# Where the sums of weight tiles are made in a split-precision encoder trunk: nine additions on GpSimd for six accumulating transfers and three VectorE additions, and three small moves before them

## The chip, the cores and the metric

The program runs on one core of a Trainium2 chip. The metric is the device time of one execution, in microseconds (us), as the median of several; a profiled execution leaves a page and a trace. The engines are TensorE (PE, with its weight loads as PEld), VectorE (DVE), ScalarE (ACT), GpSimd (POOL) and SyncE (SP). SP issues transfers only; POOL issues transfers too, those that add to their destination among them. Names such as L347 are lines of the kernel before. The changed kernel has the same lines further down: by 1 from L45, by 7 from L274 on, so that L347 is L354 there; the sums that were L296 and L306 are L276 as additions and L278 as transfers.

## The reference

A trunk of two encoder layers, for 512 tokens of width 1024, all in f32:

```
for i in range(2):
    h = rmsnorm(x, norm_g[i]);  mem_h = rmsnorm(mem, mem_norm_g[i])     # mem: 256 tokens
    if i == 0: proj = h @ w_in_a;  o_mix = dilated window attention (3 window groups, 8 heads)
    else:      proj = h @ w_in_b;  o_mix = grouped-query attention with axial rotary
    o_mem = attention of 4 heads into mem_h @ w_mem_kv[i]
    x = x + (concat(o_mix, o_mem) * silu(gate)) @ w_out[i]
```

Nearly all of its arithmetic is the product of tokens by weights: `mem_h @ w_mem_kv` first, then `h @ w_in_a` and so on.

## The kernel before

**Three products for one.** PE multiplies in a rounded f32 form (fp32r). Every operand is therefore split in a high part and the rest, a = ah + al and w = wh + wo, and each product becomes ah·wh (L178), al·wh (L179) and ah·wo (L182), added in PSUM. The first two are issued in pairs for four slices of the contraction, and then the four of L182. A weight tile `wl` of 128x1024 f32 comes by a transfer; ACT makes `wh` from it by a cast (L333), and DVE `wo = wl - wh` (L347). For the memory tokens' weights both multiply by a gain as well (L331, L345). `wh` and `wo` lie in rings of four, and the tokens' parts (`act`, `h`, `hS`) are made in the same way by L166 on ACT and L169 on DVE.

**Chunks and sums of weights.** The weights come in chunks of columns. A chunk of the token projections is computed by a Strassen scheme: instead of eight products of quarter blocks, seven, of sums of token blocks (`fS`, `hS`, L650 to L685) with sums of weight blocks 11, 12, 21, 22:

- T1 = 12 + 11, one DVE addition of two SBUF tiles (L291)
- T2 = 22 + T1, a transfer from SBUF to SBUF that adds to its destination, issued by POOL (L296)
- T3, loaded as 12, to which a second transfer from DRAM adds the block of 22, issued by POOL (L260)
- T4 = 21 + T2, again such a transfer (L306), into the tile of 21 once its parts are taken

The chunks are run in the order 1, 2, 0, 3, ...: 1 and 2 are the memory's keys and values, with four plain pieces each, and need no sums. Chunk 0 is the first Strassen chunk, with two tiles of each kind (14 weight pieces); chunk 3 is the second, with one of each (7). The pieces are used in the order 21, 11, T1, T2, 22, T3, T4.

**What sets the order.** It is written out by the program: a counter `W.g` goes up with each group of matmuls, and a weight's load, cast, low part and sums are issued once their inputs are some groups old (`ripe`). `SUM_AT` keeps the sums of chunk 0 back until group 7 (T1) and 10 (T3). The engines take their queues in order and wait on semaphores. `Driver` steps small generators for the rest: `prep` normalises the four token blocks `x[0..3]`, transposes them on PE (`first_t`, `diffs_t`) and makes their sums.

**Before the first Strassen chunk.** `place_m` transposes a memory block on PE (L589) and splits it, `square` takes the sum of squares of one, and `norm_1` takes the squares of half blocks of a token block, on ACT (L576) or DVE (L574), before POOL makes the factor `rstd` (L535, L536); `norm_2` multiplies (L583, DVE). L709 writes the memory's keys out of PSUM with their factor (DVE), L659 and L660 add a token block in PSUM to one in SBUF, and L683 and L685 subtract among tiles in SBUF.

Of the kernel before, what the change touches and what calls it, by code (L numbers as in the profile page):

```python
# [133 lines left out]
def trunk_kernel(ctx: ExitStack, tc: tile.TileContext, x, mem, wall, norm_g, mem_norm_g, gcol,  # L134
# [65 lines left out]
    class Weights:  # L200
# [61 lines left out]
        def dma(self, most=9):  # L262
            while self.allocs and self.live < KEEP_C.get(self.allocs[0][0][0], KEEP[self.allocs[0][2]]) and most:
# [6 lines left out]
                    self.at[key] = self.g  # L270
                self.load(nc.sync, self.tile[key], d)

        def ripe(self, at, key, force, n=None):
            return key in at and (force or self.g - at[key] >= (LEAD if n is None else n))  # L274

        def sum(self, force=False, want=None):  # L276

            for n, (key, d) in enumerate(self.sums[:8]):  # L278
                if want and key != want:
                    continue  # L280
                c, k, x = key
                if not c and not force and self.g < SUM_AT.get(k, 0):
                    break
                if k == "T1" and c >= T1_DMA:
                    if not self.ripe(self.load_at, key, force):
                        continue
                    self.load(G, self.tile[key], d, accum_op=ALU.add)
                elif k == "T1":
                    if not (self.ripe(self.load_at, key, force, 4 if c in KEEP_C else None) and self.ripe(self.at, (c, "11", x), force)):
                        continue  # L290
                    V.tensor_tensor(self.tile[key], self.tile[key], self.tile[c, "11", x], ALU.add)  # L291
                    self.use((c, "11", x))
                elif k == "T2":
                    if not (self.ripe(self.load_at, key, force) and self.ripe(self.at, (c, "T1", x), force, 1 if c < T1_DMA else None)):
                        continue
                    G.dma_start(self.tile[key], self.tile[c, "T1", x], accum_op=ALU.add)  # L296
                    self.use((c, "T1", x))
                elif k == "T3":
                    if not self.ripe(self.load_at, key, force):
                        continue  # L300
                    self.load(G, self.tile[key], d, accum_op=ALU.add)
                else:
                    if not (self.ripe(self.lo_at, (c, "21", x), force, 1) and self.ripe(self.at, (c, "T2", x), force, T4_AT.get(c))):
                        continue
                    self.tile[key] = self.tile[c, "21", x]
                    G.dma_start(self.tile[key], self.tile[c, "T2", x], accum_op=ALU.add)  # L306
                    self.use((c, "T2", x))
                self.at[key] = self.g
# [297 lines left out]
    def proj_t(act, sels, evac, mid=None):  # L606

        def group(w, u, b, p):
            for k in range(4):
                kk = 4 * u + k  # L610
                mm_early(p, sels[b](act, 0, kk), w[k][0], sels[b](act, 1, kk), w[k][0], kk == 0)
            if mid:
                mid(u, b)
            for k in range(4):
                kk = 4 * u + k
                mm_late(p, sels[b](act, 0, kk), w[k][1], kk == 7)
        chunk(2, len(sels), group, evac)
# [605 lines left out]
    def prep():  # L1223

        for c in range(5):
            if c > 2:
                norm_2(xb[c - 1], n[c - 1], rows["x"])
            if c == 2:
                n[2], n[3] = norm_1(xb[2], 1), norm_1(xb[3], 2)
            if 1 < c < 4:  # L1230
                first_t(H, xb[c - 2], c - 2, by_class, from_rows)
            yield 1

        def forms(c):
# [755 lines left out]
```

## Time and profile before

| | |
|---|---|
| runs | 932.94, 933.12, 933.17 us; median 933.12 |
| profiled execution | 933.17 us, span of the trace 931.4 us |
| TensorE clock granted | 1.0 |
| busy, of the span | PEld 87%, ACT 75%, POOL 39% |
| instructions | 16276 |

Times in the trace are us from the span's start; the 1.8 us between span and execution lie outside the trace. A row of the timeline has the start, the busy time, the engine with line and operation, output and inputs, shapes, a count where like instructions are drawn together, and in brackets the idle time before it with what ended that. Successive operations of one engine may overlap in it by about 0.1 us (an operation's start is less than its duration after the one before). A row of a wait has the waiting group, its releaser, and then the total us, the count and the mean.

The memory's products lie at about 8 to 32 us, chunk 0 at about 32 to 70 us, and chunk 3 after it.

### The profile page before, as it was taken

To read this page: it belongs to the slowest core of one execution; us is meant where nothing else is said; L and a number is where in the kernel's file an instruction comes from. 1 tells how busy PE (TensorE), PEld (TensorE's weight loads), DVE (VectorE), ACT (ScalarE), POOL (GpSimd) and SP (SyncE) were. 2 spreads that over 40 slices of the span, in tenths; PEclk is the share of its full clock that TensorE was granted. 3 is DMA by queue.
4 is the path that set the end of the run, shared out by engine and by line. 5 is a ranking of instruction groups with operands and counts; after the bars stand their busy time and mean duration, and the time that the engine had idled before them with its cause. 6 is when DMAs were issued, how large, how long until landed. Compare 5 with 4: busy or idle time off the path is not lost.

```text
span 931.4 us, 16276 instructions
## 1 busy us (share of the span) xinstructions
PE 924.8 (99%) x5471; PEld 814.7 (87%) x5471; DVE 801.7 (86%) x1457; ACT 695.7 (75%) x1725; POOL 360.5 (39%) x504
## 2 busy tenths in 40 slices
PE   9999999999999999999999999999999999999998
PEld 7789888888888888888889998888988999999886
DVE  6999677879888888979798989999898998789977
ACT  7775789677868686867776767757879887789774
POOL 4411425556564646464746102234252440110122
PEclk9999999999999999999999999999999999999999
DMA  9999948968686778686867899999985687785777
GB/s 351 389 264 331 300 127 218 319 146 247 162 248 166 249 160 271 159 272 135 241 178 207 231 261 271 289 320 331 289 219 114 178 233 178 201 227 116 200 162 181
DMA packets 83179, 212.85 MB, mean 229 GB/s; under 512 B 18960, under 2 KB 25752, under 8 KB 83096
## 3 DMA queue, kind: packets, MB, share of 16 engines
q1 hardware_dynamic: 60744, 141.16, 42.3%
q0 software_dynamic: 20384, 67.12, 39.1%
q10 hardware_dynamic: 1968, 3.54, 1.0%
q8 instruction: 43, 0.70, 0.3%
q14 instruction: 40, 0.33, 0.1%
HBM read 162.96 MB, written 12.65 MB: 189 GB/s over the span
## 4 chain that ended last, share of the span: by engine, by line
PE 91%; DVE 5%; DMA 2%; ACT 1%; SPq 0%; issue 0%; DVEq 0%; ACTq 0%
PE pj L178 24%; PE pj L179 24%; PE pj L182 24%; PE qT L716 3%; PE sa L1476 2%; PE oo L1585 2%; PE ptb L1819 1%; PE sa L1472 1%; DVE wo L347 1%; PE pt L1564 1%; DMA x<-in_x_dram 1%; DMA row<-in_norm_g_dram 1%; PE ob L178 1%; PE ob L182 1%; PE ob L179 1%; PE xT L589 1%
## 5 line engine op out<-in xcount | busy, mean ns | idle before, releaser
L347 DVE TENSOR_TENSOR wo<-wl,wh 128x1024 fp32r<-128x1024 f32 x253 | 308.8, 1225 | 5.6 <-ACT wh L333 5.6
L333 ACT CAST wh<-wl 128x1024 fp32r<-128x1024 f32 x253 | 267.3, 1061 | 27.5 <-PE pj L179 19.5
L178 PE MATMUL pj<-wh,hS 128*128 128x512 f32 (+1 forms) x416 | 154.5, 380 | 0.0
L179 PE MATMUL pj<-wh,hS 128*128 128x512 f32 (+1 forms) x416 | 148.9, 367 | 0.0
L178 PE MATMUL pj<-wh,h 128*128 128x512 f32 (+1 forms) x312 | 115.3, 378 | 0.0
L179 PE MATMUL pj<-wh,h 128*128 128x512 f32 (+1 forms) x312 | 111.6, 367 | 0.0
L536 POOL TENSOR_TENSOR rstd<-mse,half 128x4 f32<-128x4 f32 (+2 forms) x98 | 102.0, 1041 | 8.2
L182 PE MATMUL pj<-wo,hS 128*128 128x512 f32 (+1 forms) x416 | 99.5, 366 | 0.0
L179 PEld LDWEIGHTS pj<-wh,hS 128*128 128x128 f32 x416 | 78.7, 189 | 11.2
L178 PEld LDWEIGHTS pj<-wh,hS 128*128 128x128 f32 x416 | 78.6, 189 | 11.0
L535 POOL TENSOR_SCALAR mse<-hss 128x4 f32<-128x4 f32 (+1 forms) x88 | 45.6, 519 | 104.4 <-ACT junk L704 91.3
L182 PEld LDWEIGHTS pj<-wo,hS 128*128 128x128 f32 x416 | 72.4, 189 | 13.0 <-DVE wo L347 0.2
L704 ACT ACTIVATE junk<-sn 128x128 f32<-128x128 f32 x264 | 79.3, 310 | 3.4 <-DVE sn L428 3.4
L260 POOL DMA_DIRECT2D wl<-in_wall_dram x44 | 41.9, 982 | 95.4 <-DMA wl<-in_wall_dram 21.7
L1417 POOL TENSOR_TENSOR ta<-sn,tabs 128x128 f32<-128x128 f32 (+1 forms) x64 | 38.3, 605 | 104.0 <-DVE sn L709 80.4
L415 ACT COPY sn<-pj 128x512 f32<-128x512 f32 x122 | 67.2, 590 | 12.3 <-PE pj L182 12.3
L182 PE MATMUL pj<-wo,h 128*128 128x512 f32 (+1 forms) x312 | 74.5, 366 | 0.0
L306 POOL DMA_DIRECT2D wl<-wl x35 | 31.0, 895 | 109.2 <-DVE wo L347 48.7
L438 DVE TENSOR_TENSOR sn<-pj,sn 128x512 f32<-128x512 f32 x89 | 60.7, 683 | 6.5 <-PE pj L182 6.2
L179 PEld LDWEIGHTS pj<-wh,h 128*128 128x128 f32 x312 | 59.0, 189 | 8.4
L178 PEld LDWEIGHTS pj<-wh,h 128*128 128x128 f32 x312 | 59.0, 189 | 8.2
L296 POOL DMA_DIRECT2D wl<-wl x35 | 32.9, 964 | 78.7 <-DVE wl L291 18.9
(299 smaller groups left out, 2403.0 us busy)
## 6 DMA issues: line engine op xcount, KB each, us to landing
wl<-in_wall_dram SPq DMA_DIRECT2D x226, 512.0 KB, 7.4
wl<-wl POOLq DMA_DIRECT2D x70, 512.0 KB, 5.9
wl<-in_wall_dram POOLq DMA_DIRECT2D x48, 512.0 KB, 8.6
od<-o SPq DMA_DIRECT2D x9, 256.0 KB, 5.8
x<-in_x_dram SPq DMA_DIRECT2D x4, 512.0 KB
v0r<-sn SPq DMA_DIRECT2D x8, 256.0 KB, 8.5
v0d<-v0r SPq DMA_DIRECT2D x4, 512.0 KB
og<-od ACTq DMA_DIRECT2D x4, 512.0 KB
```

Of the source, the lines that this page charges most:

```text
L178: T.matmul(o, a, b, start=start, stop=False, skip_group_check=True)
L179: T.matmul(o, c, d, start=False, stop=False, skip_group_check=True)
L182: T.matmul(o, a, b, start=False, stop=stop, skip_group_check=True)
L260: queue.dma_start(t, wall[d], **how)
L333: A.copy(wh, self.tile[key])
L347: V.tensor_tensor(wo, self.tile[key], wh.bitcast(F32), ALU.subtract)
L415: A.copy(t_, b_)
L438: V.tensor_tensor(t_, b_, t_, ALU.subtract if q == "12" and late is None else ALU.add)
L535: G.tensor_scalar(e, ss, EPS, None, ALU.add)
L536: G.tensor_tensor(r, e, half[:, 0:n], ALU.pow)
L704: A.activation(jk, p[:, j * 128:(j + 1) * 128], AF.Square, scale=by, accum_out=ss[:, j:j + 1])
L1417: G.tensor_tensor(ta[:, 0:n], xn[:, 0:n, 0:32], ropeA[:, 0, b, s0:s0 + n], ALU.mult)
```

## The change

For the chunks 0 and 3, T1, T2 and T4 are made by an addition on POOL (`G.tensor_tensor` in the new method `add`, and in place of `V.tensor_tensor` for T1): six additions in chunk 0, three in chunk 3. The sums T3 and those of all later chunks stay as they were. Beside it there are three moves: the transposition of the second memory block goes in the first group after two pairs of matmuls instead of four (`mid` is called at k = 1 there), and ahead of a square; of the token blocks 2 and 3, block 2 now has both squares on DVE (one on ACT, one on DVE before), and block 3 both on ACT and one step of `prep` later (both on DVE before).

```
--- before.py
+++ after.py
@@ -42,6 +42,7 @@
 SEQ = [1, 2, 0] + list(range(3, len(PLAN)))
 T4_AT = {4: 4}
 T1_DMA = 15
+POOL_SUMS = 0, 3
 SUM_AT = {"T1": 7, "T3": 10}
 KEEP_C = {0: 14, 3: 14, 4: 12}
 KEEP = {"T2": 8, "T2b": 6, "W3": 10, "W1": 9, "W2": 10, "W2s": 9, "W1bs": 9, "W2c": 9, "W1b": 7, "W2b": 9, "W1o": 7}
@@ -270,6 +271,12 @@
                     self.at[key] = self.g
                 self.load(nc.sync, self.tile[key], d)
 
+        def add(self, c, t, u):
+            if c in POOL_SUMS:
+                G.tensor_tensor(t, t, u, ALU.add)
+            else:
+                G.dma_start(t, u, accum_op=ALU.add)
+
         def ripe(self, at, key, force, n=None):
             return key in at and (force or self.g - at[key] >= (LEAD if n is None else n))
 
@@ -288,12 +295,12 @@
                 elif k == "T1":
                     if not (self.ripe(self.load_at, key, force, 4 if c in KEEP_C else None) and self.ripe(self.at, (c, "11", x), force)):
                         continue
-                    V.tensor_tensor(self.tile[key], self.tile[key], self.tile[c, "11", x], ALU.add)
+                    (G if c in POOL_SUMS else V).tensor_tensor(self.tile[key], self.tile[key], self.tile[c, "11", x], ALU.add)
                     self.use((c, "11", x))
                 elif k == "T2":
                     if not (self.ripe(self.load_at, key, force) and self.ripe(self.at, (c, "T1", x), force, 1 if c < T1_DMA else None)):
                         continue
-                    G.dma_start(self.tile[key], self.tile[c, "T1", x], accum_op=ALU.add)
+                    self.add(c, self.tile[key], self.tile[c, "T1", x])
                     self.use((c, "T1", x))
                 elif k == "T3":
                     if not self.ripe(self.load_at, key, force):
@@ -303,7 +310,7 @@
                     if not (self.ripe(self.lo_at, (c, "21", x), force, 1) and self.ripe(self.at, (c, "T2", x), force, T4_AT.get(c))):
                         continue
                     self.tile[key] = self.tile[c, "21", x]
-                    G.dma_start(self.tile[key], self.tile[c, "T2", x], accum_op=ALU.add)
+                    self.add(c, self.tile[key], self.tile[c, "T2", x])
                     self.use((c, "T2", x))
                 self.at[key] = self.g
                 self.sums.pop(n)
@@ -609,8 +616,8 @@
             for k in range(4):
                 kk = 4 * u + k
                 mm_early(p, sels[b](act, 0, kk), w[k][0], sels[b](act, 1, kk), w[k][0], kk == 0)
-            if mid:
-                mid(u, b)
+                if mid and k == (1 if (u, b) == (0, 0) else 3):
+                    mid(u, b)
             for k in range(4):
                 kk = 4 * u + k
                 mm_late(p, sels[b](act, 0, kk), w[k][1], kk == 7)
@@ -1225,8 +1232,8 @@
         for c in range(5):
             if c > 2:
                 norm_2(xb[c - 1], n[c - 1], rows["x"])
-            if c == 2:
-                n[2], n[3] = norm_1(xb[2], 1), norm_1(xb[3], 2)
+            if 1 < c < 4:
+                n[c] = norm_1(xb[c], 2 * (c == 2))
             if 1 < c < 4:
                 first_t(H, xb[c - 2], c - 2, by_class, from_rows)
             yield 1
@@ -1311,8 +1318,8 @@
     def ahead(u, b):
 
         if (u, b) == (0, 0):
+            place_m(1, 0)
             square(1, 0)
-            place_m(1, 0)
             square(0, 1, False)
             W.hi(True)
             W.hi(True)
```

On POOL's queue, behind the last of the key factors (L770) and ahead of the sums of the third Strassen chunk, before (`wl` with a number is one weight tile; 204 and 206 are 21 of chunk 0, 208 and 210 are 11, 212 and 214 are T1, 216 and 218 are T2, 323 and 325 are T3; from 422 or 434 on they are chunk 3's):

```order
L770 TENSOR_SCALAR rstd_426<-rstd_426,rm_74 128x4
L296 DMA wl_216<-wl_212 128x1024
L296 DMA wl_218<-wl_214 128x1024
L260 DMA wl_323<-in_wall_dram 128x1024
L260 DMA wl_325<-in_wall_dram 128x1024
L306 DMA wl_204<-wl_216 128x1024
L306 DMA wl_206<-wl_218 128x1024
L296 DMA wl_572<-wl_570 128x1024
L260 DMA wl_643<-in_wall_dram 128x1024
L306 DMA wl_434<-wl_572 128x1024
L296 DMA wl_891<-wl_821 128x1024
```

and now:

```order
L298 TENSOR_TENSOR wl_212<-wl_212,wl_208 128x1024
L298 TENSOR_TENSOR wl_214<-wl_214,wl_210 128x1024
L276 TENSOR_TENSOR wl_216<-wl_216,wl_212 128x1024
L276 TENSOR_TENSOR wl_218<-wl_218,wl_214 128x1024
L261 DMA wl_323<-in_wall_dram 128x1024
L261 DMA wl_325<-in_wall_dram 128x1024
L276 TENSOR_TENSOR wl_204<-wl_204,wl_216 128x1024
L276 TENSOR_TENSOR wl_206<-wl_206,wl_218 128x1024
L298 TENSOR_TENSOR wl_570<-wl_570,wl_424 128x1024
L276 TENSOR_TENSOR wl_572<-wl_572,wl_570 128x1024
L261 DMA wl_643<-in_wall_dram 128x1024
L276 TENSOR_TENSOR wl_422<-wl_422,wl_572 128x1024
```

Six issues of transfers are gone from the queue and nine additions in their place; the issues of T3 (L260, now L261) stand behind four additions now, and T1's additions are the first work of the queue there.

On DVE, from the last normalisation of the token blocks on (`xn` are the memory's keys, `wo` the low parts of weight pieces), before:

```order
L583 SCALAR_TENSOR_TENSOR x<-x,rstd,row 128x512 x2
L709 TENSOR_TENSOR xn<-pj,rstd 128x512
L347 TENSOR_TENSOR wo<-wl,wh 128x1024 x2
L709 TENSOR_TENSOR xn<-pj,rstd 128x512
L291 TENSOR_TENSOR wl<-wl 128x1024
L659 TENSOR_TENSOR fS_532<-xT,f_496 128x512
L660 TENSOR_TENSOR fS_533<-f_402,xT 128x512
L169 TENSOR_TENSOR hS_536<-fS_532,hS_536 128x4x128
L347 TENSOR_TENSOR wo<-wl,wh 128x1024 x2
L291 TENSOR_TENSOR wl<-wl 128x1024
L659 TENSOR_TENSOR fS_574<-xT,f_537 128x512
L660 TENSOR_TENSOR fS_575<-f_456,xT 128x512
```

and now:

```order
L590 SCALAR_TENSOR_TENSOR x<-x,rstd,row 128x512 x2
L716 TENSOR_TENSOR xn<-pj,rstd 128x512
L354 TENSOR_TENSOR wo<-wl,wh 128x1024 x2
L716 TENSOR_TENSOR xn<-pj,rstd 128x512
L666 TENSOR_TENSOR fS_532<-xT,f_496 128x512
L667 TENSOR_TENSOR fS_533<-f_390,xT 128x512
L170 TENSOR_TENSOR hS_536<-fS_532,hS_536 128x4x128
L354 TENSOR_TENSOR wo<-wl,wh 128x1024 x2
L666 TENSOR_TENSOR fS_574<-xT,f_537 128x512
L667 TENSOR_TENSOR fS_575<-f_456,xT 128x512
L170 TENSOR_TENSOR hS_536<-fS_574,hS_536 128x4x128
L354 TENSOR_TENSOR wo<-wl,wh 128x1024
```

The two L291 of chunk 0 are gone; every other operation keeps its place. (A third L291, chunk 3's, is gone further on.)

On ACT, where the weight pieces of the memory end (`sq` are squares of a token half block, `h` the high parts of tokens, `junk` squares of memory keys), before:

```order
L331 ACTIVATE wh<-wl,gmc 128x512 x4
L576 ACTIVATE sq,ss<-x 128x512
L166 CAST h_389<-xT 128x4x128
L166 CAST h_395<-xT 128x4x128
L650 COPY f_400<-xT 128x512
L650 COPY f_402<-xT 128x512
L704 ACTIVATE junk,hss<-pj,rm 128x128 x4
L166 CAST h_389<-xT 128x4x128
L166 CAST h_395<-xT 128x4x128
```

and now:

```order
L338 ACTIVATE wh<-wl,gmc 128x512 x4
L167 CAST h_377<-xT 128x4x128
L167 CAST h_383<-xT 128x4x128
L657 COPY f_388<-xT 128x512
L657 COPY f_390<-xT 128x512
L711 ACTIVATE junk,hss<-pj,rm 128x128 x4
L583 ACTIVATE sq,ss<-x 128x512 x2
L167 CAST h_377<-xT 128x4x128
L167 CAST h_383<-xT 128x4x128
```

The cast of the first token block moves ahead of the square, which now stands, with a second one, behind four of the `junk` operations.

More of the change, by code (lines that the diff above doesn't have):

```diff
@@ L44 @@
 T1_DMA = 15
+POOL_SUMS = 0, 3
 SUM_AT = {"T1": 7, "T3": 10}
@@ L271, in dma, with add @@
                 self.load(nc.sync, self.tile[key], d)
+        def add(self, c, t, u):
+            if c in POOL_SUMS:
+                G.tensor_tensor(t, t, u, ALU.add)
+            else:
+                G.dma_start(t, u, accum_op=ALU.add)
         def ripe(self, at, key, force, n=None):
@@ L290, in sum @@
                         continue
-                    V.tensor_tensor(self.tile[key], self.tile[key], self.tile[c, "11", x], ALU.add)
+                    (G if c in POOL_SUMS else V).tensor_tensor(self.tile[key], self.tile[key], self.tile[c, "11", x], ALU.add)
                     self.use((c, "11", x))
@@ L295, in sum @@
                         continue
-                    G.dma_start(self.tile[key], self.tile[c, "T1", x], accum_op=ALU.add)
+                    self.add(c, self.tile[key], self.tile[c, "T1", x])
                     self.use((c, "T1", x))
@@ L305, in sum @@
                     self.tile[key] = self.tile[c, "21", x]
-                    G.dma_start(self.tile[key], self.tile[c, "T2", x], accum_op=ALU.add)
+                    self.add(c, self.tile[key], self.tile[c, "T2", x])
                     self.use((c, "T2", x))
@@ L611, in group @@
                 mm_early(p, sels[b](act, 0, kk), w[k][0], sels[b](act, 1, kk), w[k][0], kk == 0)
-            if mid:
-                mid(u, b)
+                if mid and k == (1 if (u, b) == (0, 0) else 3):
+                    mid(u, b)
             for k in range(4):
@@ L1227, in prep @@
                 norm_2(xb[c - 1], n[c - 1], rows["x"])
-            if c == 2:
-                n[2], n[3] = norm_1(xb[2], 1), norm_1(xb[3], 2)
+            if 1 < c < 4:
+                n[c] = norm_1(xb[c], 2 * (c == 2))
             if 1 < c < 4:
@@ L1313, in ahead @@
         if (u, b) == (0, 0):
+            place_m(1, 0)
             square(1, 0)
-            place_m(1, 0)
             square(0, 1, False)
```

## The prediction

> **What bounds the kernel.** I read the page first: the busy times and the chain of waits by engine.
>
> ```profile
> PE 924.8 (99%) x5471; PEld 814.7 (87%) x5471; DVE 801.7 (86%) x1457; ACT 695.7 (75%) x1725; POOL 360.5 (39%) x504
> PE 91%; DVE 5%; DMA 2%; ACT 1%; SPq 0%; issue 0%; DVEq 0%; ACTq 0%
> ```
>
> TensorE (PE) works 924.8 of 931.4 us and 91% of the chain is PE, so time is won only where PE stands still, and a time that PE loses is not given back. Next, who PE's weight loads and matmuls waited for, over the whole run:
>
> ```profile
> PE xT L589 <- DVE x L583: 1.0, 1, 1.0
> PEld xT L589 <- issue: 1.3, 1, 1.3
> PEld pj L179 <- DVE act L169: 1.3, 3, 0.6
> PEld pj L178 <- ACT wh L331: 0.8, 2, 0.5
> ```
>
> The first two rows are one place, the transposition of the input tokens at 31.64 us, late by 1.0 us (1.3 at the weight load); the other two lie before 15 us. Then the busy time in the stretch that the change touches, in the columns PE, weight load, VectorE (DVE), ScalarE (ACT), GpSimd (POOL):
>
> ```profile
> 34.00:46.00 12.00, 12.00 (x59) 10.01 (x58) 11.69 (x14) 8.41 (x13) 2.88 (x4) 1.00 1.04 378
> 46.00:58.00 12.00, 12.00 (x58) 9.80 (x57) 11.80 (x15) 9.80 (x16) 2.61 (x3) 1.00 1.06 245
> 82.00:94.00 12.00, 12.00 (x103) 12.00 (x102) 8.87 (x11) 6.05 (x15) 3.09 (x4) 1.00 1.05 342
> ```
>
> From 34 to 58 us PE has no hole and DVE rests 0.31 and 0.20 us of 12; only from 82 us on has DVE room (8.87 of 12). How close DVE runs behind PE there, by the timeline:
>
> ```profile
> 53.52 1.22 DVE L347 TENSOR_TENSOR wo<-wl,wh 128x1024 fp32r<-128x1024 f32 x1
> 54.82 1.16 PE L182 MATMUL pj<-wo,hS 128*128 128x512 f32 x4
> ```
>
> The low part `wo` of the seventh weight piece of chunk 0 is ready at 53.52 + 1.22 = 54.74 and PE takes it at 54.82: a margin of 0.08 us. **PE is the bound, and DVE stands right behind it just where the change puts new work on POOL.**
>
> **What the change costs and brings, part by part.**
>
> *The squares and the transposition, before 32 us.* Of the squares of the last two token blocks, one less is on DVE, and the last block's come later, on ACT.
>
> ```profile
> 10.91 0.50 PE L179 MATMUL pj<-wh,act 128*128 128x512 f32 x1 [0.23 <-DVE act L169]
> 22.38 2.62 ACT L331 ACTIVATE wh<-wl,gmc 128x512 fp32r<-128x512 f32 x4 [0.96 <-DMA wl<-in_wall_dram]
> 24.86 0.69 DVE L574 CUSTOM_DVE_ANT_0 sq<-x 128x512 f32<-128x512 f32 x1 [1.10 <-DMA x<-in_x_dram]
> 25.52 1.05 ACT L166 CAST h<-xT 128x512 fp32r<-128x512 f32 x2
> 31.64 1.06 PE L589 MATMUL xT<-ident,x 128*128 128x128 f32 x8 [1.03 <-DVE x L583]
> ```
>
> DVE waited 1.10 us for the last block's transfer before a square, and ACT's cast at 25.52 stood behind a square. Both go: DVE loses the wait and one 0.6 us square, but what it does next needs ACT's cast, which moves up from 25.52 to 25.0 only (ACT's weight casts end there: 22.38 + 2.62). So DVE's queue, and the block that PE waits for at 31.64, come 0.5 to 0.6 us earlier. The two squares on ACT (0.8 each with their read-out) push its next casts to about 30.9; DVE needs them at 31, so they cost nothing. The earlier transposition of a memory block lets ACT and DVE make its tokens sooner; PE waited 0.23 us for such a one at 10.91, but what it wins there it only waits longer at 31.64: the last wait decides. Taken: **-0.6 us**; bounds 0 and -2.4 (every wait above gone).
>
> *Transfers that go.* Nine additions were six accumulating transfers on POOL's queue and three DVE additions.
>
> ```profile
> 52.49 1.05 ACT L333 CAST wh<-wl 128x1024 fp32r<-128x1024 f32 x1 [0.75 <-DMA wl<-wl]
> ```
>
> ACT waited 0.75 us for one such sum, and PE had no hole meanwhile (the row of 46 to 58 us). Worth nothing; bounds 0 and, at most, that 0.75.
>
> *Nine additions of 128x1024 on POOL.* The trace has none of that size; the nearest rows are POOL's products of 128x64 and 128x128:
>
> ```profile
> 178.32 0.46 POOL L1417 TENSOR_TENSOR ta<-sn,tabs 128x128 f32<-128x128 f32 x1 [3.59 <-DVE sn L709]
> 178.74 1.54 POOL L1418 TENSOR_TENSOR tb<-sn,tabs 128x128 f32<-128x128 f32 x1
> 178.75 1.22 DVE L347 TENSOR_TENSOR wo<-wl,wh 128x1024 fp32r<-128x1024 f32 x1
> 179.88 1.48 DVE L291 TENSOR_TENSOR wl<-wl 128x1024 f32<-128x1024 f32 x1
> 199.05 0.68 DVE L438 TENSOR_TENSOR sn<-pj,sn 128x512 f32<-128x512 f32 x1
> 199.21 0.32 POOL L1417 TENSOR_TENSOR ta<-sn,tabs 128x64 f32<-128x64 f32 x1 [3.88 <-DVE sn L709]
> 203.66 1.33 DVE L347 TENSOR_TENSOR wo<-wl,wh 128x1024 fp32r<-128x1024 f32 x1 [1.01 <-ACT wh L333]
> ```
>
> Alone, 64 elements take 0.32 and 128 take 0.46 us: 2.2 ns an element, so 1024 take 0.46 + 896 x 0.0022 = **2.4 us** (an estimate; below it nothing but the 0.46 of the row). The middle rows tell more. L1418 met L347, whose two inputs both lie in SBUF, and took 1.54 instead of 0.46 us: it waited until L347 was done. Then L291, also with two SBUF inputs, took 1.48 instead of 1.22 us: it waited 0.26 us for L1418. So the two exclude each other, for 0.26 / 128 = 2.03 ns an element. L438, whose second input is in PSUM, took its 0.68 us beside a POOL product: it isn't held. For 1024 elements the hold is 2.03 ns x 1024 = **2.08 us**; bounds 0.26 (the lock goes back to DVE piece by piece, and DVE's reads fit between) and 2.4 (the whole instruction).
>
> [...]
>
> *Where the holds fall.* What POOL did and does there:
>
> ```profile
> 31.61 0.60 POOL L770 TENSOR_SCALAR rstd<-rstd,rm 128x4 f32<-128x4 f32 x2
> 38.83 1.08 POOL L296 DMA_DIRECT2D wl<-wl  x1 [6.62 <-DVE wl L291]
> 44.77 2.11 POOL L260 DMA_DIRECT2D wl<-in_wall_dram  x2
> wl<-in_wall_dram POOLq DMA_DIRECT2D x48, 512.0 KB, 8.6
> ```
>
> POOL is free from about 33 us (the row's 32.2, plus the moved norm factor). Before, it then waited 6.62 us for DVE's sum. Now it can start at once, and the next eight additions run back to back, with the two issues of L260 (about 1 us each) after the fourth. Behind those issues stand two pieces of T3: at 2.4 and the 1.1 that an addition waits for an L347, they go out at 33 + 4 x 3.5 = 47 us instead of 44.77, and land 8.6 us later by the median; PE, itself late, takes them after the pieces of T1, T2 and 22, past 58 us. I cost that at nothing (without PE's delay, 2 us). What DVE has to do in the same stretch:
>
> ```profile
> 33.82 0.69 DVE L709 TENSOR_TENSOR xn<-pj,rstd 128x512 f32<-128x512 f32 x1
> 34.42 2.35 DVE L347 TENSOR_TENSOR wo<-wl,wh 128x1024 fp32r<-128x1024 f32 x2
> 36.69 0.69 DVE L709 TENSOR_TENSOR xn<-pj,rstd 128x512 f32<-128x512 f32 x1
> 37.29 1.22 DVE L291 TENSOR_TENSOR wl<-wl 128x1024 f32<-128x1024 f32 x1
> 38.42 0.69 DVE L659 TENSOR_TENSOR fS<-xT,f 128x512 f32<-128x512 f32 x1
> 39.02 0.68 DVE L660 TENSOR_TENSOR fS<-f,xT 128x512 f32<-128x512 f32 x1
> 39.80 0.69 DVE L169 TENSOR_TENSOR hS<-fS,hS 128x512 fp32r<-128x512 f32 x1
> 40.41 2.35 DVE L347 TENSOR_TENSOR wo<-wl,wh 128x1024 fp32r<-128x1024 f32 x2
> 46.13 1.23 DVE L347 TENSOR_TENSOR wo<-wl,wh 128x1024 fp32r<-128x1024 f32 x1 [0.26 <-ACT wh L333]
> 47.28 0.68 DVE L683 TENSOR_TENSOR f<-fS,f 128x512 f32<-128x512 f32 x1
> 48.00 0.69 DVE L685 TENSOR_TENSOR f<-f,f 128x512 f32<-128x512 f32 x1
> ```
>
> If, as at 179.88, the one that waits is let in next, one DVE operation with two SBUF inputs passes between two additions. In order: first addition while L709 (PSUM) runs; L347; second; L347; third, beside L709, L659 and L660 (PSUM); L169; fourth; L347; POOL's two issues, beside them L347; fifth, beside L659 and L660; L169; sixth; L347; seventh; L683; eighth; L685. All eight holds thus fall ahead of the `wo` at 53.52. The sum for DVE there:
>
> - eight holds: 8 x 2.08 = +16.6 us
> - covered by operations on PSUM: 0.6 + 1.8 + 1.2 = -3.6
> - two removed L291, 37.29 to 38.42 each: -2.3
> - DVE's rests of 0.31 and 0.20 in the stretch: -0.5
> - DVE enters earlier by the squares: -0.5
> - margin of 54.82: -0.1
>
> **+9.6 us** for PE, which already contains the -0.6: PE waits for DVE whatever it won before. The chunk's later pieces have wider margins, and the third removed L291 (after 58 us) and the ninth addition (after 73 us, where DVE comes to rest) change nothing. Against the profiled execution's 933.17 (span 931.4 and 1.8 around it; the median of the runs is 933.12): 933.2 + 9.6 = **942.8 us**. With holds of 2.4 it is 945.3; if all eight PSUM operations of that stretch cover (another 1.2) and three holds fall in DVE's gaps, 936.
>
> **Rivals.**
> 1. *No lock that counts.* At 1024 elements POOL reads in pieces and DVE's reads go between, so that an addition costs DVE no more than the 0.26 us of the small one: 8 x 0.26 = 2.1, less than the 2.3 of the removed L291. PE keeps the 0.6 us: 933.2 - 0.6 = 932.6, not slower. For it: no row here is longer than 128 elements. Against it: the hold doubles from 64 to 128 elements (L347 grew by 0.11 at 203.66 beside the small form, L291 by 0.26 beside the large). It decides where a hold is under (2.3 + 3.6 + 1.1) / 8 = 0.9 us, by the terms above.
> 2. *Shared by halves.* The two alternate within an addition, each hold costs DVE half, 1.04 us: 8.3 - 1.8 (cover by halves) - 2.3 - 1.1 = +3.1: 936.3.
> 3. *Faster.* The lock does not count, and fewer transfers bring the weights so early that every later wait of PE goes as well: 933.2 - 0.6 and 1.5 for them = 931.1. Against: none of the groups of waits above names a transfer.
> 4. *The sums don't move at all.* The rows of the order ahead have the additions on POOL and DVE's L291 gone there, so this gets no chance.
>
> **Chances and range.** Forecast 0.68; rival 1: 0.16; rival 2: 0.10; rival 3: 0.06. A measurement of this kernel can tell about 0.2%, 1.9 us, from no change. Faster by more: rival 3, 0.06. Within: rival 1, 0.16. Slower by more: 0.68 + 0.10 = 0.78. The likeliest case alone spans 936 to 946 us (holds of 2.4 and 0.7 for starts that drift); with it and rival 2 alone too much would be left out, so the range reaches down to rival 1: 932.3 to 946.
>
> **What would show it.** Right: L347 (now L354) between 34 and 58 us on average near 2.3 us instead of 1.22, single ones above 3; POOL's additions 2.4 us alone and up to 3.5 where they wait; PE waiting for DVE's `wo` by some 10 us in total before 65 us, the largest single wait 3 to 5 us; DVE without idle time; and from 65 us on the same PE pace as before, later by 9 to 10 us. The start right: PE's wait at 31.64 comes 0.5 earlier. Wrong: L354 stays at 1.22 us beside additions of 2.4 (rival 1), or grows by about 1 us (rival 2). Most of all it would be wrong if DVE is let in more often than one operation per addition.

## The result: 946.4 to 946.9 us, 1.4% slower

| | forecast | measured |
|---|---|---|
| time | 942.8 us (932.3 to 946.0) | 946.91 us median of 4, before 933.14 in the same runs |
| ratio to before | 1.010 | 1.0144 (95% interval 1.0126 to 1.0162) |
| the same kernel once more | | 946.42 us, ratio 1.0138 (1.0121 to 1.0155) |

The direction and the mechanism were right; the loss is 13.8 us where 9.6 were forecast, and the time lies 0.9 us above the range. One of the four executions, the profiled one, took 2386 us, with the matmuls of 512 columns 0.62 us apart instead of 0.23 (without it the median is 946.35), so the profile read here is that of the second series, an execution of 946.61 us with a span of 944.6.

The stretches that the prediction quoted, now (columns as there: PE, weight load, VectorE, ScalarE, GpSimd, then the granted clock of TensorE):

```profile
34.00:46.00 12.00, 9.37 (x43) 6.87 (x41) 11.91 (x7) 6.18 (x10) 12.00 (x6) 1.00 0.98 392
46.00:58.00 12.00, 6.65 (x17) 4.52 (x17) 11.90 (x6) 2.18 (x4) 11.92 (x7) 0.64 0.52 95
58.00:70.00 12.00, 12.00 (x46) 9.71 (x47) 11.93 (x16) 9.79 (x15) 0.24 (x1) 0.79 0.59 140
82.00:94.00 12.00, 12.00 (x75) 10.83 (x75) 11.70 (x11) 6.05 (x8) 3.28 (x2) 1.00 0.67 211
```

VectorE is busy for 11.9 of each 12 us in the first two stretches (11.69 and 11.80 before), but the number of its operations fell from 14 and 15 to 7 and 6: it stands in them. TensorE loses 2.63 us in the first stretch and 5.35 in the second, and its clock, 1.00 throughout before, is 0.64 and 0.79 from 46 to 70 us. The waits of TensorE by groups show whom it waited for:

```profile
PE pj L183 <- DVE wo L354: 7.0, 2, 4.5
PEld pj L183 <- DVE wo L354: 8.3, 3, 4.9
```

Before, no row of the matmuls' waits named `wo`, and the rows of the weight loads came to 0.5 us for it in the whole run; now the low products (ah·wo) wait 7.0 us for it. On VectorE (L354 was L347, L170 was L169, L666 was L659):

```profile
33.92 6.16 DVE L354 TENSOR_TENSOR wo<-wl,wh 128x1024 fp32r<-128x1024 f32 x2
41.97 0.92 DVE L170 TENSOR_TENSOR hS<-fS,hS 128x512 fp32r<-128x512 f32 x1
42.81 3.38 DVE L354 TENSOR_TENSOR wo<-wl,wh 128x1024 fp32r<-128x1024 f32 x1
46.11 9.07 DVE L354 TENSOR_TENSOR wo<-wl,wh 128x1024 fp32r<-128x1024 f32 x1
55.11 0.68 DVE L666 TENSOR_TENSOR fS<-xT,f 128x512 f32<-128x512 f32 x1
56.48 1.50 DVE L170 TENSOR_TENSOR hS<-fS,hS 128x512 fp32r<-128x512 f32 x1
```

and on GpSimd, the eight additions and the two issues between them:

```profile
32.87 6.13 POOL L298 TENSOR_TENSOR wl<-wl 128x1024 f32<-128x1024 f32 x2
38.95 6.15 POOL L276 TENSOR_TENSOR wl<-wl 128x1024 f32<-128x1024 f32 x2
45.05 2.04 POOL L261 DMA_DIRECT2D wl<-in_wall_dram  x2
46.45 5.35 POOL L276 TENSOR_TENSOR wl<-wl 128x1024 f32<-128x1024 f32 x2
51.12 2.98 POOL L298 TENSOR_TENSOR wl<-wl 128x1024 f32<-128x1024 f32 x1
54.17 3.25 POOL L276 TENSOR_TENSOR wl<-wl 128x1024 f32<-128x1024 f32 x1
```

Two L354 that met the first additions took 6.16 us instead of 2.35, L170 took 0.92 and 1.50 instead of 0.69, and L666, with its input in PSUM, the same 0.68 as ever. One L354 took **9.07 us**: it was shut out by the fifth, sixth and seventh addition in a row (46.45 to 54.10).

Where the time stands lost. For each kernel that was run, the table has the start of the first low product of a weight piece, less the same start in the kernel before (from the rows of TensorE in the two traces; the pieces are those that the kernel before starts at 34.39, the last of the memory, 43.45, 46.17, 48.89, 54.82, 71.70 and 106.41 us):

| kernel | 34.39 | 43.45 | 46.17 | 48.89 | 54.82 | 71.70 | 106.41 |
|---|---|---|---|---|---|---|---|
| the change | -0.82 | +2.79 | +9.07 | +12.61 | +13.37 | +13.29 | +13.29 |
| additions alone | -0.21 | +12.70 | +14.91 | +14.94 | +14.93 | +14.85 | +14.85 |
| moves alone | -0.57 | -0.58 | -0.58 | -0.55 | -0.29 | -0.25 | +0.25 |
| chunk 3's three alone | -0.90 | -0.91 | -0.91 | -0.89 | -0.61 | +2.36 | +2.54 |
| chunk 0's six alone | -0.87 | +2.78 | +6.76 | +10.30 | +10.66 | +10.58 | +10.58 |
| holes filled | -0.86 | +3.15 | +9.42 | +10.97 | +11.70 | +11.74 | +11.74 |
| T3 behind the seventh | -0.66 | +2.97 | +3.58 | +6.99 | +12.34 | +12.24 | +12.25 |
| additions in halves | -0.79 | -0.30 | -0.15 | +11.74 | +13.51 | +13.43 | +13.43 |
| T1 on VectorE | -1.04 | -1.04 | -1.04 | +5.60 | +7.36 | +8.01 | +8.56 |
| T1 by transfers | -0.97 | -0.97 | -0.97 | -0.97 | -0.12 | +6.21 | +8.05 |
| squares alone | -1.09 | -1.09 | -1.09 | -1.08 | -0.82 | -0.51 | -0.22 |
| transposition alone | +0.78 | +0.77 | +0.77 | +0.77 | +0.77 | +0.77 | +1.33 |

In the change everything is lost between 34 and 55 us of the kernel before, and from there on TensorE keeps its pace, 13.29 us behind.

### The profile page after: what moved, and what is told of

Same layout as the page of the kernel before. It is cut to its first block, busy times and chain, and to the rows that moved or that the text cites. A ratio compares the mean times of both kernels' runs of the same rounds, so it can differ in the third digit from the quotient of the medians.

```text
span 2384.0 us, 16280 instructions
## 1 busy us (share of the span) xinstructions
PE 2379.3 (100%) x5471; PEld 1712.6 (72%) x5471; DVE 809.6 (34%) x1452; ACT 714.2 (30%) x1727; POOL 331.3 (14%) x507
## 4 chain that ended last, share of the span: by engine, by line
PE 100%; DVE 0%; DVEq 0%; issue 0%; POOL 0%; POOLq 0%
PE pj L180 26%; PE pj L183 26%; PE pj L179 26%; PE qT L723 3%; PE ptb L1826 2%; PE sa L1483 2%; PE oo L1592 2%; PE sa L1479 1%; PE pt L1571 1%; PE xT L596 1%; PE ob L180 1%; PE ob L179 1%; PE ob L183 1%; PE sb L174 1%; PE sb L173 1%; PE sb L175 1%
## 5 line engine op out<-in xcount | busy, mean ns | idle before, releaser
L354 DVE TENSOR_TENSOR wo<-wl,wh 128x1024 fp32r<-128x1024 f32 x253 | 309.3, 1225 | 113.3 <-ACT wh L340 81.7
L179 PE MATMUL pj<-wh,hS 128*128 128x512 f32 (+1 forms) x416 | 328.1, 790 | 0.0
L180 PE MATMUL pj<-wh,hS 128*128 128x512 f32 (+1 forms) x416 | 315.1, 759 | 0.0
L179 PE MATMUL pj<-wh,h 128*128 128x512 f32 (+1 forms) x312 | 245.3, 787 | 0.0
L183 PE MATMUL pj<-wo,hS 128*128 128x512 f32 (+1 forms) x416 | 240.9, 761 | 0.0
L180 PE MATMUL pj<-wh,h 128*128 128x512 f32 (+1 forms) x312 | 236.8, 760 | 0.0
L179 PEld LDWEIGHTS pj<-wh,hS 128*128 128x128 f32 x416 | 155.3, 373 | 68.0 <-issue 59.6
L180 PEld LDWEIGHTS pj<-wh,hS 128*128 128x128 f32 x416 | 155.6, 374 | 65.2 <-issue 65.2
L183 PEld LDWEIGHTS pj<-wo,hS 128*128 128x128 f32 x416 | 143.3, 375 | 77.1 <-issue 73.5
L183 PE MATMUL pj<-wo,h 128*128 128x512 f32 (+1 forms) x312 | 180.3, 759 | 0.0
L180 PEld LDWEIGHTS pj<-wh,h 128*128 128x128 f32 x312 | 117.4, 376 | 49.1 <-issue 49.0
L179 PEld LDWEIGHTS pj<-wh,h 128*128 128x128 f32 x312 | 118.0, 378 | 48.1 <-issue 44.7
L183 PEld LDWEIGHTS pj<-wo,h 128*128 128x128 f32 x312 | 107.7, 372 | 58.0 <-issue 56.7
L422 ACT COPY sn<-pj 128x512 f32<-128x512 f32 x122 | 69.6, 589 | 175.7 <-PE pj L183 175.7
L542 POOL TENSOR_SCALAR mse<-hss 128x4 f32<-128x4 f32 (+1 forms) x88 | 34.3, 390 | 612.3 <-ACT junk L711 600.7
L179 PE MATMUL pj<-hS,wh 128*128 128x256 f32 x192 | 105.4, 555 | 0.0
L180 PE MATMUL pj<-hS,wh 128*128 128x256 f32 x192 | 100.9, 531 | 0.0
```

What stands on the lines that cost most here:

```text
L179: T.matmul(o, a, b, start=start, stop=False, skip_group_check=True)
L180: T.matmul(o, c, d, start=False, stop=False, skip_group_check=True)
L183: T.matmul(o, a, b, start=False, stop=stop, skip_group_check=True)
L354: V.tensor_tensor(wo, self.tile[key], wh.bitcast(F32), ALU.subtract)
L422: A.copy(t_, b_)
```

## The experiments

**The change again, and its two halves.** The first expectation is that of the changed kernel's second series; "Theory L" and "Theory C" are used from here on. Where the expectations speak of a port, the runs show only that an addition on GpSimd and a VectorE operation with two SBUF inputs keep each other waiting (two L354 6.16 us instead of 2.35, above); what lies behind that was not shown.

> The changed kernel once more, for a profile at its usual pace (its first profile caught an execution of 2386 us, in which every matmul took more than twice its time). Theory L, the shared port alone: 946 to 947 us; VectorE is held once for each of eight additions, about 2.1 us each, and TensorE's waits for wo between 34 and 80 us add up to the whole 13.4 us. Theory C, the port and then TensorE's clock: the other runs of this kernel show a granted clock of 0.992 where the kernel before has 1.0, so TensorE's waits add up to only 9 to 10 us, and the other 3 to 4 us lie in matmuls that stand further apart after a wait, in windows with a granted clock below 1.00.

Measured: 946.42 us. Both theories had a part of it. TensorE's holes over 0.15 us up to 60 us add up to 10.2 us (2.23 in the kernel before), so 7.9 us are standing time; the rest of the 13.3 is slow work. Around the two holes, from TensorE's timeline:

```profile
46.24 2.08 PE L183 MATMUL pj<-wo,h 128*128 128x512 f32 x4 [2.47 <-DVE wo L354]
55.24 2.07 PE L183 MATMUL pj<-wo,h 128*128 128x512 f32 x4 [4.50 <-DVE wo L354]
58.51 0.63 PE L180 MATMUL pj<-wh,hS 128*128 128x512 f32 x1
58.94 0.63 PE L179 MATMUL pj<-wh,hS 128*128 128x512 f32 x1
```

and the granted clock in short stretches (the number after the parenthesis of GpSimd):

```profile
46.00:48.00 2.00, 1.76 (x4) 1.48 (x5) 2.00 (x2) 0.00 (x0) 2.00 (x3) 0.51 0.77 113
48.00:50.00 2.00, 2.00 (x7) 1.54 (x7) 2.00 (x1) 0.00 (x0) 2.00 (x2) 0.64 1.00 199
50.00:52.00 2.00, 0.74 (x4) 0.27 (x2) 2.00 (x1) 0.00 (x0) 2.00 (x2) 1.00 1.06 203
52.00:54.00 2.00, 0.00 (x0) 0.00 (x0) 2.00 (x1) 0.00 (x0) 2.00 (x1) 0.71 0.30 57
54.00:62.00 8.00, 6.15 (x14) 4.37 (x15) 7.87 (x9) 5.05 (x7) 4.16 (x3) 0.50 0.39 62
62.00:64.00 2.00, 2.00 (x8) 1.63 (x7) 1.97 (x4) 1.14 (x2) 0.00 (x0) 0.73 0.08 14
64.00:66.00 2.00, 2.00 (x11) 1.59 (x10) 2.00 (x4) 2.00 (x4) 0.00 (x0) 1.00 0.49 185
```

Inside the hole that ends at 55.24 the clock falls to half; four low products take 2.07 us instead of 1.16, matmuls start 0.43 us apart (58.51, 58.94) instead of 0.23, and the clock is back only at about 63. By the rows, half clock lasts (1 - 0.71) x 2 / 0.5 = 1.2 us of 52 to 54, all of 54 to 62, and 1.1 us of 62 to 64: 10.2 us. With the hole of 2.47 us the clock fell to half as well, and for a shorter time: by the 0.51 and 0.64 of the first two rows of 2 us from 46 on, (0.49 + 0.36) x 2 / 0.5 = 3.4 us.

> The nine additions on GpSimd alone; squares and transposition as before. Both theories: 946.5 to 947.5 us, at most 0.6 above the whole change, since the earlier start of VectorE is worth no more than 0.6. If the moves and not the additions made the loss, it would come out near 933.

```diff
-                if mid and k == (1 if (u, b) == (0, 0) else 3):
+                if mid and k == 3:
...
-            if 1 < c < 4:
-                n[c] = norm_1(xb[c], 2 * (c == 2))
+            if c == 2:
+                n[2], n[3] = norm_1(xb[2], 1), norm_1(xb[3], 2)
...
+            square(1, 0)
             place_m(1, 0)
-            square(1, 0)
```

Measured: 948.27 us, ratio 1.0162 (1.0147 to 1.0177), 1.85 above the whole change where at most 0.6 was expected. So the additions make the loss, and the moves save a part of it. On VectorE the additions now meet the last normalisation of the token blocks (L590, L583 before, both inputs in SBUF): 5.41 us for two instead of 1.41, and TensorE waits 3.7 us for the blocks that come of it:

```profile
32.29 5.41 DVE L590 SCALAR_TENSOR_TENSOR x<-x,rstd,row 128x512 f32<-128x512 f32 x2
PE xT L596 <- DVE x L590: 3.7, 2, 2.7
```

> The squares and the transposition moved, all sums as before. Both theories: 932.5 us, 0.6 below the kernel before, with TensorE's wait for the token block near 31.6 us shorter by 0.5. If the moves cost time, 933.5 or more.

```diff
-POOL_SUMS = 0, 3
+POOL_SUMS = ()
```

Measured: nine executions of 933.0 to 937.8 us and one of 1312.46, median of the ten 935.81, ratio 1.0018 (1.0004 to 1.0031). By the table TensorE is 0.58 us ahead from 34 to 49 us, as the prediction had it, gives back half of that at the piece at 54.82, and the rest and 0.25 more near 104 us, at a wait that was not taken apart. The weight load of the piece at 54.82:

```profile
53.26 1.22 DVE L354 TENSOR_TENSOR wo<-wl,wh 128x1024 fp32r<-128x1024 f32 x1
54.53 0.76 PEld L183 LDWEIGHTS pj<-wo,hS 128*128 128x128 f32 x4 [0.52 <-DVE wo L354]
```

TensorE comes 0.29 us earlier than before and its weight load still waits 0.52 for VectorE: the margin of 0.08 us is used up. Of the executions above 935 us there is no trace; they have a mean granted clock of 0.997 to 0.999.

> Only the moved squares; transposition and sums as before. If the squares set the wait near 31.6 us: TensorE 0.5 earlier there, given back at 54.8 by VectorE, 932.8 to 933.4. If they do nothing: 933.1 and the wait at 31.6 unchanged.

```diff
-POOL_SUMS = 0, 3
+POOL_SUMS = ()
...
-                if mid and k == (1 if (u, b) == (0, 0) else 3):
+                if mid and k == 3:
...
+            square(1, 0)
             place_m(1, 0)
-            square(1, 0)
```

> Only the earlier transposition of the second memory block; squares and sums as before. It waits for its block's transfer, near 8 us, so a hole of 0.3 to 0.9 us opens in the first group; it wins the 0.23 us at 10.9, and the wait at 31.6 takes the difference: 933.1. If the early hole lets TensorE's clock start later: executions of 935 to 938, as some of the moves together show.

```diff
-POOL_SUMS = 0, 3
+POOL_SUMS = ()
...
-            if 1 < c < 4:
-                n[c] = norm_1(xb[c], 2 * (c == 2))
+            if c == 2:
+                n[2], n[3] = norm_1(xb[2], 1), norm_1(xb[3], 2)
```

Measured: squares alone 933.72 us, ratio 1.0019 (1.0003 to 1.0036), transposition alone 933.70, ratio 1.0005 (0.9996 to 1.0015). In the traces, the squares take the whole wait of 1.03 us near 31.6 away (TensorE 1.09 ahead, twice what was expected) and TensorE gives most of it back in three steps of about 0.27 us, at 54.82, at 71.70 and near 104. The executions of 937 to 940 us (four of ten, mean clock 0.996 to 0.998) come with the squares and not, as expected, with the transposition, none of whose ten is above 934.8; why stays open. The transposition waits for its block's transfer and wins nothing (in its trace, an execution of 934.53 us, it loses 0.77).

**Which additions cost.**

> The whole change, but only the three additions of chunk 3 on GpSimd; chunk 0 sums as before. Theory L: three holds of 2.1 to 2.4 us less one removed VectorE addition of 1.2, against margins of 1 to 4 us of the pieces there and the 0.6 of the moves: 932.5 to 937 us. Theory C the same, and a granted clock of 1.00, since no wait of TensorE is longer than 2 us. If most of the loss sat in chunk 3, it would be over 940.

```diff
-POOL_SUMS = 0, 3
+POOL_SUMS = (3,)
```

> Only the six additions of chunk 0 on GpSimd; chunk 3 as before. VectorE's longest hold covers two additions instead of three. Theory L alone: two holds of 2.1 to 2.4 less (the seventh and eighth addition) and one VectorE addition of 1.2 more: 943 to 944. [...]

```diff
-POOL_SUMS = 0, 3
+POOL_SUMS = (0,)
```

> The whole change with T1 of both chunks left on VectorE: six additions on GpSimd. Five of them lie ahead of the piece that decides (before: at 54.82 us). By a price of 2.4 us an addition, three fewer are worth 7.1 and two T1 on VectorE cost 2.3 again: 11.7 - 7.1 + 2.3 = 6.9 us of lateness without the clock, 940 to 941.5 with up to 1.5 of it. If the loss came from T1 alone (from their meeting the first weight pieces): 934 to 936. If the T2 and T4 alone make it: 944 or more.

```diff
-                    (G if c in POOL_SUMS else V).tensor_tensor(self.tile[key], self.tile[key], self.tile[c, "11", x], ALU.add)
+                    V.tensor_tensor(self.tile[key], self.tile[key], self.tile[c, "11", x], ALU.add)
```

Measured: 937.15 us with three additions (ratio 1.0041, 1.0026 to 1.0056), 942.01 with six that leave out T1 (1.0095, 1.0080 to 1.0110), 944.03 with the six of chunk 0 (1.0116, 1.0101 to 1.0131), 946.42 with nine. With three additions, just above the 937 that were expected at most, the two holds of VectorE are these, after which TensorE stands 2.7 us (expected: under 2) and its clock stays at 1.00:

```profile
54.07 2.90 DVE L681 TENSOR_TENSOR hS<-f,hS 128x512 fp32r<-128x512 f32 x1
56.89 3.38 DVE L354 TENSOR_TENSOR wo<-wl,wh 128x1024 fp32r<-128x1024 f32 x1
58.00:70.00 12.00, 9.67 (x43) 8.00 (x44) 12.00 (x13) 8.64 (x12) 2.00 (x2) 1.00 1.07 285
PE pj L183 <- DVE wo L354: 2.7, 1, 2.7
```

With T1 on VectorE, TensorE is 7.36 us late at the piece at 54.82, where 6.9 without the clock were worked out and up to 1.5 more with it. But four additions and not five lie ahead of that piece (they start at 37.86, 44.29, and two from 48.03 on):

```profile
39.06 1.75 DVE L170 TENSOR_TENSOR hS<-fS,hS 128x512 fp32r<-128x512 f32 x1
45.50 1.74 DVE L170 TENSOR_TENSOR hS<-fS,hS 128x512 fp32r<-128x512 f32 x1
47.16 7.27 DVE L354 TENSOR_TENSOR wo<-wl,wh 128x1024 fp32r<-128x1024 f32 x1
```

VectorE loses 1.06, 1.05 and 6.05 us in them, 8.2 in all or 2.0 an addition, against 14.86 / 8 = 1.9 in the change (worked out below); so nothing here sets the additions of T1 apart from those of T2 and T4. With chunk 0's six alone the time fits the 943 to 944 of Theory L, although the clock did fall as Theory C has it (mean 0.994, with matmuls 0.43 us apart from 48.11 on). The next expectation puts the price of the clock at about 5 us; its run shows that there was no such sum to win.

**The clock by itself.**

> The changed kernel with 14 and 28 additional matmuls of zeros by zeros (128x128) on TensorE, ahead of the low products of the third and the fourth piece of chunk 0, where the profile of the changed kernel has TensorE idle for 2.47 and 4.50 us; at 0.13 us each (eight transpositions take 1.06) they fill 1.9 and 3.7 us of these holes and change no result. Theory C (the clock falls to half after such a hole, and that costs time of its own): TensorE's granted clock stays at 1.00, and the time falls by the work that ran at half clock, about 5 us, to 941 to 942. Theory L (only VectorE's lateness counts): 946.4 as before, since the holes end when wo is ready.

```diff
+FILL = {11: 14, 12: 28}
...
+                for _ in range(FILL.get(W.taken, 0)):
+                    T.matmul(bank[s][0][:, 0:128], zero, zero, start=False, stop=False, skip_group_check=True)
                 for b, k, kk, bs, o in regions():
```

```profile
46.00:58.00 12.00, 10.86 (x81) 9.85 (x79) 11.90 (x6) 2.19 (x4) 11.92 (x7) 1.00 0.50 92
58.00:70.00 12.00, 11.65 (x53) 9.12 (x54) 11.93 (x16) 10.03 (x16) 0.23 (x1) 1.00 0.60 144
46.07 9.10 DVE L355 TENSOR_TENSOR wo<-wl,wh 128x1024 fp32r<-128x1024 f32 x1
55.60 1.17 PE L184 MATMUL pj<-wo,h 128*128 128x512 f32 x4
57.91 0.50 PE L180 MATMUL pj<-wh,hS 128*128 128x512 f32 x1 [1.14 <-ACT sn L423]
```

and the same place in the change:

```profile
57.92 0.79 PE L179 MATMUL pj<-wh,hS 128*128 128x512 f32 x1 [0.61 <-ACT sn L422]
```

Measured: 945.02 us, ratio 1.0126 (1.0111 to 1.0141). The clock stays at 1.00 and VectorE's holds are the same (9.10), so this is the price of the holds alone: 11.74 us. The filling itself takes a little more than the holes (the low products start at 55.60, 0.43 us after `wo` at 46.07 + 9.10 = 55.17), but that costs nothing: in both kernels TensorE then waits for a copy on ScalarE (L423, L422 in the change) and goes on at 57.9. The clock's own part is 13.29 - 11.74 = **1.55 us** in the traces, 1.4 in the medians, not 5: the slow work ahead of 57.9 lay where TensorE would have waited for `wo` or for that copy all the same, and what is left is eight matmuls behind it, 0.43 us apart instead of 0.23. Both theories were off, and the truth lies between them.

**How additions and VectorE take turns.**

> The changed kernel with the two issues of T3 moved on GpSimd's queue from behind the fourth addition to behind the seventh. In the changed kernel the additions 5, 6 and 7 stand behind these issues, start each 0.69 us before the end of the one ahead and let no VectorE operation in between, and one low part of a weight piece takes 9.07 us. Theory B (GpSimd runs ahead of itself behind an issue of a transfer and so keeps the port over several additions): additions 1 to 7 now alternate with VectorE, the longest VectorE operation is about 3.4 us, TensorE's longest hole at most 3.5 us, and the time 941 to 945. Rival: the additions keep the port whenever a next one is ready; then operations of over 5 us stay, and the time is 945 to 948.

```diff
-SUM_AT = {"T1": 7, "T3": 10}
+SUM_AT = {"T1": 7, "T3": 14}
...
                 if not c and not force and self.g < SUM_AT.get(k, 0):
+                    if k == "T3":
+                        continue
                     break
```

```profile
39.13 12.81 POOL L276 TENSOR_TENSOR wl<-wl 128x1024 f32<-128x1024 f32 x4
42.99 6.71 DVE L356 TENSOR_TENSOR wo<-wl,wh 128x1024 fp32r<-128x1024 f32 x2
52.41 3.42 DVE L356 TENSOR_TENSOR wo<-wl,wh 128x1024 fp32r<-128x1024 f32 x1
```

Measured: 945.57 us, ratio 1.0131 (1.0114 to 1.0147). With the issues out of the way the additions 3 to 6 take 3.2 us each, and VectorE's L356 (L354) passes between them at 3.4 us each; nothing takes 9 us, and TensorE's longest hole is 3.36. That part of Theory B holds. But the time is only 0.9 us lower, above its 941 to 945: VectorE's operations lose 14.7 us over the stretch against 14.9 in the change (sums of the durations less 1.22 or 0.69 each). Alternation spreads the loss and takes nothing off it. The eighth addition is still behind the two issues here, and by itself it costs a VectorE operation 3.96 - 0.69 = 3.27 us:

```profile
55.75 3.96 DVE L692 TENSOR_TENSOR f<-fS,f 128x512 f32<-128x512 f32 x1
56.10 3.06 POOL L276 TENSOR_TENSOR wl<-wl 128x1024 f32<-128x1024 f32 x1
```

> Each of the nine additions as two of 128x512. Theory L by whole instructions: a VectorE operation that meets one waits at most 1.1 to 1.2 us instead of 2.4, and one passes after each half, so VectorE loses half as much while GpSimd takes twice as many turns: the low parts in the stretch take about 2.4 us, TensorE's holes are under 3 us and 938 to 943 us come out. If the port is kept over several instructions whatever their size: 945 to 948.

```diff
-                G.tensor_tensor(t, t, u, ALU.add)
+                for h in (slice(0, 512), slice(512, 1024)):
+                    G.tensor_tensor(t[:, h], t[:, h], u[:, h], ALU.add)
```

(T1 goes through the same method.)

```profile
32.90 14.83 POOL L277 TENSOR_TENSOR wl<-wl 128x512 f32<-128x512 f32 x8
40.79 4.53 DVE L358 TENSOR_TENSOR wo<-wl,wh 128x1024 fp32r<-128x1024 f32 x2
49.06 10.43 POOL L277 TENSOR_TENSOR wl<-wl 128x512 f32<-128x512 f32 x8
48.20 12.38 DVE L358 TENSOR_TENSOR wo<-wl,wh 128x1024 fp32r<-128x1024 f32 x1
```

Measured: 947.53 us, ratio 1.0153 (1.0138 to 1.0168). Ahead of the two issues (47.66) both expectations of whole instructions come true: L358 (L354) takes 2.27 us, held 1.05 by a half, and TensorE is even 0.15 us ahead at the piece at 46.17. Behind them eight halves run in a row and one L358 takes 12.38 us. So a run of additions behind the issues kept VectorE out in halves (12.38 us) as it did whole (9.07).

The runs together show what is special behind the issues. In the kernel with chunk 0's six alone two additions stand behind them, and L354 meets both:

```profile
46.10 6.77 DVE L354 TENSOR_TENSOR wo<-wl,wh 128x1024 fp32r<-128x1024 f32 x1
```

One addition behind the issues costs the waiting operation 3.27 us, two 6.77 - 1.22 = 5.55, three 7.85: each further one 2.3, hardly more than the 2.2 of one in alternation. The surplus of 1.0 us is there once (1.4 with T1 on VectorE, 6.05 for two, where the operation came earlier). VectorE's operation gets nothing done from its own start on, which is 0.35 us (T3 behind, 55.75) and 0.86 us (halves, 48.20) ahead of the first addition's recorded start, while the issues are still on GpSimd: with the halves it ends 1.09 us, nearly its whole own time, after the last of them (48.20 + 12.38 against 49.06 + 10.43). Issues with no addition behind them held nothing in the kernel before (L347 at 46.13 took 1.23 us beside the row of L260 at 44.77).

**VectorE relieved without additions on GpSimd.**

> The moves of squares and transposition, and T1 of the chunks 0 and 3 by an accumulating transfer between SBUF tiles, as T2 and T4 are in the kernel before; no addition on GpSimd and no T1 on VectorE. VectorE is relieved of two operations of 1.2 us before 54.8 us without anything on GpSimd's port. If VectorE's margin of 0.08 us at 54.82 is what gave back the 0.6 us that the moves alone won before 34 us: TensorE stays 0.5 to 0.6 ahead there, and the time is 932.3 to 932.8. Rival: the three transfers more come late or take from the weight loads, and a new wait of TensorE makes it 933.5 or more.

```diff
-POOL_SUMS = 0, 3
+POOL_SUMS, T1_SUMS = (), (0, 3)
...
-                    (G if c in POOL_SUMS else V).tensor_tensor(self.tile[key], self.tile[key], self.tile[c, "11", x], ALU.add)
+                    if c in T1_SUMS:
+                        G.dma_start(self.tile[key], self.tile[c, "11", x], accum_op=ALU.add)
+                    else:
+                        V.tensor_tensor(self.tile[key], self.tile[key], self.tile[c, "11", x], ALU.add)
```

```profile
51.22 1.05 ACT L343 CAST wh<-wl 128x1024 fp32r<-128x1024 f32 x1 [2.93 <-DMA wl<-wl]
55.51 1.05 ACT L343 CAST wh<-wl 128x1024 fp32r<-128x1024 f32 x1 [2.73 <-DMA wl<-wl]
```

Measured: 941.37 us, ratio 1.0087 (1.0072 to 1.0102): the rival. T2 now waits for the landing of one transfer before its own is issued (7.51 and 3.89 us on GpSimd's queue, ahead of the issues at 42.22 and 46.98), and ScalarE's casts wait 2.93 and 2.73 us for the sums. TensorE keeps its 0.97 us until 49 us and has lost it at 54.82; the 6 us at 71.70 fall in chunk 3, with a hole of 3.46 us (the mean clock of the span is 0.996), and were not taken apart.

None of the kernels beats the one before.

## Why the prediction was right and wrong

- **What bounds the kernel: right.** VectorE, with its 0.08 us of margin at 54.82, decided in the change and also in the moves alone, where at that piece it took half of the gain back.
- **Nine additions of 2.4 us: right.** An addition that meets nothing takes 2.40 us, as with T1 on VectorE:

```profile
37.86 2.40 POOL L276 TENSOR_TENSOR wl<-wl 128x1024 f32<-128x1024 f32 x1 [5.18 <-DVE wl L298]
```

- **Who is held: right.** L354 (up to 9.07 us instead of 1.22), L170 (up to 1.50 instead of 0.69) and L590 (5.41 instead of 1.41 for two, with the additions alone) are; L716, L666 and L667, with an input in PSUM (0.68, 0.67 and 0.67 us beside the addition that starts at 38.95), are not.
- **Eight holds of 2.08 us: too small in sum.** The step that failed is the term of eight holds, 16.6 us less 3.6 of cover, 13.0 us. VectorE lost 14.86 us in the six rows quoted above (3.81, 0.23, 2.16, 7.85 and 0.81 us over their usual time, L666 nothing), 1.86 more. Most of that lies behind the issues: the first four additions cost 6.20 us where the same terms give 4 x 2.08 - 2.4 = 5.9, and the last four 7.85 + 0.81 = 8.66 where they give 4 x 2.08 - 1.2 = 7.1. In alternation an L354 that waited for a whole addition lost 2.2 us, so the 2.08 worked out from the small form was nearly right; behind the issues L354 lost 7.85 in three additions, 2.6 each. With holds of 2.4 us, its upper bound, the prediction's sum gave 945.3; the kernel without the fall of the clock took 945.02. That agreement is partly luck: the 2.2 us lie below the 2.4 of the bound, and the surplus behind the issues makes up for it.
- **One VectorE operation between two additions: right for the first four, wrong for the next three,** which stand behind two issues of transfers. The run cost nothing by itself: with the issues moved, VectorE lost 14.7 us.
- **The terms taken off (removed L291, rests, earlier start, margin: 3.4 us): right as a sum.** 14.86 - 3.4 = 11.46, and 11.7 was measured where the clock stayed up. The terms were not measured one by one; the earlier start alone was 0.57 us with the moves alone. The low end of the likeliest case is not the 936 that was written: its terms give 942.8 - 1.2 - 3 x 2.08 = 935.4.
- **The clock: left out.** The prediction quoted a granted clock of 1.00 and forecast holes of 3 to 5 us, and didn't ask what holes do to it. That is 1.55 us more. With 2.1 for the holds (11.7 instead of 9.6) it makes the 3.7 us that were missing in the trace: 13.3 instead of 9.6.
- **The squares: right in size at first** (0.6 to 1.1 us at 34 us), but rival 1's "PE keeps the 0.6" was wrong: it is given back by 106 us, half of it to VectorE at 54.82. Beside the additions the moves were worth 1.85 us, since they bring L590 ahead of the first addition.
- **What would show it: right in its main points.** The waits for `wo` were 7.0 to 8.3 us instead of some 10, the largest 4.5; L354 held up to 9.07 where "above 3" was said, and 4.65 on average over the four of 34 to 56 us where 2.3 was said; later by a constant amount from 55 us on, but by 13.3 us and not 9 to 10. The remark that it would be wrong most of all if VectorE were let in more often had the side wrong: it was let in less often.

## What to carry to other kernels

Before work goes from VectorE or a transfer to GpSimd, count the SBUF inputs on both sides: with VectorE full (11.69 and 11.80 of 12 us before), each GpSimd addition of 2.4 us here cost it 1.9 us on average and 2.2 in alternation, and the VectorE operations that ran beside it at their usual 0.68 us were those with an input in PSUM. The transfers of the kernel before, whose waits were hidden, cost TensorE nothing (it was busy for 12.00 of each 12 us there), and to replace them by additions of 2.4 us that shut VectorE out was a loss (15.1 us with the additions alone), however idle GpSimd looked (39% busy). When a change opens holes on TensorE, ask for the clock behind them too (0.50 here with the hole of 4.50 us), and count of its slow work only what does not end in another wait (1.55 us here).

## What the runs showed of the hardware

- Additions on GpSimd behind two issues of transfers run without a gap that VectorE can use: with three of 128x1024 one operation took 9.07 us, with eight of 128x512 one took 12.38. Without the issues ahead, they alternate with VectorE one by one (3.4 and 2.27 us for the VectorE operation). Their starts show it: the seventh starts at 51.12, 0.68 us before the fifth and sixth end (46.45 + 5.35), where the third starts at 38.95 and the pair before it ends at 39.00. The price of an addition is about the same both ways (2.3 and 2.2 us); what an issue adds is 1.0 to 1.4 us once, ahead of the first addition. Why an issue has this effect wasn't tried further.
- The exclusion goes both ways. With T1 on VectorE, an addition that met a row of VectorE operations took 6.81 us instead of 2.40:

```profile
68.29 6.81 POOL L276 TENSOR_TENSOR wl<-wl 128x1024 f32<-128x1024 f32 x1 [14.95 <-PE pj L180]
```

- Whether a hole of TensorE brings the clock down is not told by its length alone: with the hole of 2.47 us before 46.24 the clock fell to half in the change, with one of 2.49 us at the same place (T3 behind) and one of 2.65 us (chunk 3's three alone) it did not. With the holes of 4.50 and 8.12 us (additions alone) the clock was at half for 10.2 us each time, and in the change TensorE was at work for about 7 of them; with the hole of 10.46 us (halves) the mean clock of the span was 0.994, as with the additions alone.
